# State space branch: the order in program text of a group's norm (third) and the turning of the next group's features (turn)

## The chip, the cores and the metric

The kernel runs on one core of a Trainium2 chip. The metric is the device time of one execution in microseconds (us). An execution is the whole program: two transformer-like layers of a first block and one layer of a second block on 512 tokens of width 1024, in float32.

## The reference, cut to what matters

The change lies in the state space branch of the second block. For 8 groups of 4 heads (head width 64, state width 128, chunks of 128 tokens) the branch computes a decayed, causal sum forwards and backwards, adds a skip term, multiplies by a gate and takes a root-mean-square norm over the 256 features of each group.

```python
def ssd_branch(z, xbc, dt_raw, conv_w, conv_b, dt_bias, a_log, d_skip, norm_g):
    xbc = jax.nn.silu(depthwise_conv_centred(xbc, conv_w, conv_b)).astype(f32)
    xs = xbc[..., :D_INNER].reshape(b, l, SSD_HEADS, SSD_HEAD_DIM)
    Bm = ...; Cm = ...
    y_fwd = ssd_chunked(xs, dt[:, :, 0], A[0], Bm, Cm)
    y_bwd = fl(ssd_chunked(fl(xs), fl(dt[:, :, 1]), A[1], fl(Bm), fl(Cm)))
    y = y_fwd + y_bwd + d_skip.astype(f32)[:, None] * xs
    y = y.reshape(b, l, D_INNER) * jax.nn.silu(z.astype(f32))
    yg = y.reshape(b, l, SSD_GROUPS, D_INNER // SSD_GROUPS)
    yg = yg * lax.rsqrt(jnp.mean(yg * yg, axis=-1, keepdims=True) + EPS)
    y = yg.reshape(b, l, D_INNER) * norm_g.astype(f32)
```

Its result is multiplied by `w_ssd_branch`. Every large product is made of three matmuls on numbers that are split into a rounded high part and a low part.

## The kernel before, in words

All of the work of a stage is written in one text, and a scheduler places every instruction on its engine. It walks a timeline of its own; among instructions that are ready, what stands earlier in the text goes first. So the order of two calls in the text is a preference, and the order on the engines is fixed once the program is built. Each engine then works through its own list strictly in that order, and waits where an operand or a buffer is not there yet.

The branch is written as a class `Group` with five steps, for group g = 0 to 7:

- `feats` (L1267): projections of the group's features from XTh and XTl (matmuls L457 to L459 into a psm bank), and a convolution of each of the four results. The convolution is one ScalarE pass (L1253), four VectorE passes (L1257) and a Silu (L1259).
- `turn` (L1290): for each of four chunks, three TensorE transposes (L1302 twice, L1303) into one pss bank, and two ScalarE copies (L1304 for s.x, L1305 for s.Bt).
- `first` (L1336): four products B times C into the bank s.cb (L1343), then the states. A step of a state is a VectorE product (L1310), a matmul into a pss bank (L1312) and a decayed sum on VectorE (four of L1319, or one copy L1315). `decays` fetches a table of decays by a DMA that GpSimd issues (L1327, into ab), adds and masks it on VectorE (L1329, L1330), takes exponentials on ScalarE (L1332) and multiplies by s.cb (L1333).
- `gate`, `second` (L1358): for each chunk c, matmuls L1368, L1370 and L1381, the sums on VectorE (L1371 to L1382), the product with the gate (L1383), and its squares' sum on ScalarE (L1384). L1384 also overwrites the last use of the chunk's ab buffer, so the next group's DMA into that buffer follows it.
- `third` (L1386): the mean (L510, VectorE), the power -1/2 (L506, GpSimd), four products (L1392), eight transposes (L1394) into two pss banks pts, and the split of both banks (L468 on ScalarE, L469 on VectorE).

There are three psm banks and five pss banks, and a pss bank is given to the next taker when its last reader is done. The branch's output product (L625 adds it to ACC, or L623 copies it) is written behind `feats` of every second group as `ssd_out`, and for the last pair as `ssd_out_group(6)` and `(7)`. Weights come by DMA from SyncE, and are split by L165 (ScalarE) and L167 (VectorE). When `turn` and `third` are called is set by the loop at L1415 to L1429.

Of the kernel before, what the change touches and what calls it, by code (L numbers as in the profile page):

```python
# [246 lines left out]
def body(ctx, tc, I, out, dbg=None, stop=None):  # L247
# [349 lines left out]
    def tok2(w, src, evac, n_k=8):  # L597

        for t in range(NT):
            ps = PM()  # L600
            tk = slice(t * P, (t + 1) * P)
            for k in range(n_k):
                xh, xl = src(k)
                mm3(ps, (xh[:, tk], xl[:, tk]), w[k], k == 0, k == n_k - 1)
            evac(t, ps)
# [15 lines left out]
    def add_to(dst, ps, first):  # L621
        if first:
            nc.scalar.activation(out=dst, in_=ps, func=AF.Copy)  # L623
        else:
            nc.vector.tensor_tensor(out=dst, in0=ps, in1=dst, op=ALU.add)  # L625
# [334 lines left out]
    for j in range(4):  # L960
        heads = []
        for hh in range(2):
            hd = 2 * j + hh
            Z = wk.get("Z", 1024, 4)
            G = wk.get("G", 512, 4)
# [432 lines left out]
    def ssd_out(i):  # L1398
        for u in range(2):
            tok2(WT.get(f"so{i}{u}"), uk, lambda t, ps: add_to(acc[:, t, u * 512:(u + 1) * 512], ps, i == 0), n_k=4)  # L1400

    def ssd_out_group(g):
        for u in range(2):
            w = WT.get(f"so3{g}{u}")
            for t in range(NT):
                ps = PM()
                tk = slice(t * P, (t + 1) * P)
                for k in range(2):
                    uh, ul = uk((2 * g + k) % 4)
                    mm3(ps, (uh[:, tk], ul[:, tk]), w[k], k == 0, k == 1)  # L1410
                add_to(acc[:, t, u * 512:(u + 1) * 512], ps, False)

    G = [Group(g) for g in range(8)]
# [3 lines left out]
    for g in range(8):  # L1417
        G[g].first()
        G[g].gate()
        G[g].second()  # L1420
        if g < 7:
            G[g + 1].feats()
        else:
            ssd_out_group(6)
        if g in (2, 4, 6):
            ssd_out(g // 2 - 1)
        if g < 7:
            G[g + 1].turn()
        G[g].third()  # L1429
    ssd_out_group(7)  # L1430
    for t in range(NT):
        nc.gpsimd.dma_start(h[:, t], hD[t * P:(t + 1) * P, :])
# [238 lines left out]
def kernel_body(tc, I, out, dbg=None, stop=None):  # L1671
    with ExitStack() as ctx:
        body(ctx, tc, I, out, dbg, stop)
# [25 lines left out]
```

## Time and profile before

| what | value |
|---|---|
| time, median of 3 runs | 2582.27 us (2581.29 to 2585.32) |
| the profiled execution's own time | 2581.83 us |
| its span | 2580.1 us |
| TensorE busy, mean granted clock | 2504.9 us (97%), 0.989 |
| VectorE busy | 1714.5 us (66%) |
| ScalarE busy | 1220.2 us (47%) |
| state space branch, from the first table of decays to group 7's norm | about 1357 to 1793 us |
| idle TensorE in 1357 to 1793 us, by the list of waits | 22.5 us |

The span is what the trace covers; the execution's own time is 1.7 us more. Busy is the time in which an engine works on an instruction. A busy TensorE isn't one at full speed: the clock that was granted is listed for each stretch, and 0.50 means 1.2 GHz in place of 2.4 GHz. The matmuls are pipelined, so the distance of two starts tells what one costs.

### The profile page before, as it was taken

What the parts mean: (1) busy time and instruction counts of PE and PEld (TensorE: products, weight loads), DVE (VectorE), ACT (ScalarE), POOL (GpSimd) and SP (SyncE); (2) the same over time, 40 slices, a digit from 0 to 9 for tenths busy, and PEclk for the clock granted to TensorE, in tenths of its full rate; (3) what the DMA queues carried; (4) which work ended last, traced back from release to release, by engine and by line L of the source; (5) the groups of instructions that cost most, each with busy time, mean ns of one, the idle gap of its engine ahead of it and who ended that gap; (6) DMA issues with size and microseconds to landing.
All of it is one profiled execution on the core that took longest, in us unless ns stands there. A gap on an engine that the chain in (4) does not pass through costs nothing. (4 is left out here: it accounts for less than half of the span.)

```text
span 2580.1 us, 33650 instructions
## 1 busy us (share of the span) xinstructions
PE 2504.9 (97%) x12848; PEld 2088.2 (81%) x12848; DVE 1714.5 (66%) x3048; ACT 1220.2 (47%) x2181; POOL 183.5 (7%) x199
## 2 busy tenths in 40 slices
PE   8999999999999989999999999998999999999998
PEld 7888888778888768877888788787887789878877
DVE  5566567775566657577477788887555466487674
ACT  6333345443476554444356554563455436444342
POOL 1100220000201030000121100010000000100000
PEclk9999999999999989999999999998999999999999
DMA  5521235333232133453334333352221233243441
GB/s 175 162 66 61 87 115 169 125 108 129 82 96 89 63 97 113 140 179 98 102 109 125 106 104 109 104 148 77 73 67 40 84 113 123 82 147 104 141 139 58
DMA packets 202001, 278.11 MB, mean 108 GB/s; under 512 B 10800, under 2 KB 127776, under 8 KB 201840
## 3 DMA queue, kind: packets, MB, share of 16 engines
q1 hardware_dynamic: 190352, 236.29, 29.4%
q0 software_dynamic: 10192, 34.96, 5.0%
q10 hardware_dynamic: 1296, 4.72, 0.5%
q8 instruction: 101, 1.65, 0.3%
q14 instruction: 60, 0.49, 0.1%
HBM read 271.56 MB, written 9.61 MB: 109 GB/s over the span
## 5 line engine op out<-in xcount | busy, mean ns | idle before, releaser
L458 PE MATMUL psm<-XTl,hl 128*128 128x512 f32 (+1 forms) x1400 | 537.3, 384 | 7.8 <-DVE XTl L466 7.8
L457 PE MATMUL psm<-XTh,hl 128*128 128x512 f32 (+1 forms) x1400 | 534.5, 382 | 5.9 <-ACT XTh L465 5.1
L459 PE MATMUL psm<-XTh,hl 128*128 128x512 f32 (+1 forms) x1400 | 533.3, 382 | 0.0
L165 ACT ACTIVATE hl<-raw 128x1024 fp32r<-128x1024 f32 x303 | 319.3, 1056 | 313.9 <-PE psm L459 132.6
L167 DVE TENSOR_TENSOR hl<-raw,hl 128x1024 fp32r<-128x1024 f32 x287 | 352.7, 1233 | 149.0 <-ACT hl L165 147.9
L458 PEld LDWEIGHTS psm<-XTl,hl 128*128 128x128 f32 x1400 | 266.3, 190 | 56.9 <-DVE XTl L466 8.6
L457 PEld LDWEIGHTS psm<-XTh,hl 128*128 128x128 f32 x1400 | 265.9, 190 | 55.7 <-ACT XTh L465 6.1
L459 PEld LDWEIGHTS psm<-XTh,hl 128*128 128x128 f32 x1400 | 266.3, 190 | 48.5
L457 PE MATMUL psm<-hl,XTh 128*128 128x512 f32 (+1 forms) x640 | 231.1, 362 | 4.4 <-ACT XTh L465 3.3
L458 PE MATMUL psm<-hl,XTh 128*128 128x512 f32 (+1 forms) x640 | 229.9, 359 | 0.1
L459 PE MATMUL psm<-hl,XTl 128*128 128x512 f32 (+1 forms) x640 | 229.1, 358 | 0.0
L457 PE MATMUL psm<-hl,UAh 128*128 128x512 f32 x368 | 148.6, 405 | 4.9 <-DVE ACC L625 1.5
L458 PE MATMUL psm<-hl,UAh 128*128 128x512 f32 x368 | 144.9, 395 | 0.0
L459 PE MATMUL psm<-hl,UAl 128*128 128x512 f32 x368 | 143.7, 396 | 0.0
L457 PEld LDWEIGHTS psm<-hl,XTh 128*128 128x128 f32 x640 | 122.3, 191 | 21.8 <-ACT XTh L465 3.7
L458 PEld LDWEIGHTS psm<-hl,XTh 128*128 128x128 f32 x640 | 122.2, 191 | 16.6 <-issue 0.5
L459 PEld LDWEIGHTS psm<-hl,XTl 128*128 128x128 f32 x640 | 122.3, 191 | 15.9 <-issue 0.5
L671 ACT ACTIVATE WK<-psm 128x512 f32<-128x512 f32 x66 | 39.5, 598 | 160.8 <-PE psm L459 160.8
L457 PE MATMUL psm<-hl,UBh 128*128 128x512 f32 (+1 forms) x240 | 93.5, 391 | 1.1 <-ACT UBh L468 0.8
L459 PE MATMUL psm<-hl,UBl 128*128 128x512 f32 (+1 forms) x248 | 94.3, 388 | 0.0
L1257 DVE SCALAR_TENSOR_TENSOR WS<-psm,CW,WS 128x511 f32<-128x511 f32 (+1 forms) x120 | 87.5, 740 | 8.7 <-ACT WS L1253 8.4
L458 PE MATMUL psm<-hl,UBh 128*128 128x512 f32 (+1 forms) x240 | 92.2, 386 | 0.0
(481 smaller groups left out, 4839.2 us busy)
## 6 DMA issues: line engine op xcount, KB each, us to landing
raw<-in_mlp_w_down_dram SPq DMA_DIRECT2D x76, 512.0 KB, 3.3
raw<-in_mlp_w_up_dram SPq DMA_DIRECT2D x64, 512.0 KB, 3.9
raw<-in_w_in_dram SPq DMA_DIRECT2D x60, 512.0 KB, 3.7
raw<-in_w_down_dram SPq DMA_DIRECT2D x38, 512.0 KB, 3.9
WS<-aD POOLq DMA_DIRECT2D x32, 512.0 KB, 5.9
raw<-in_w_up_dram SPq DMA_DIRECT2D x32, 512.0 KB, 3.7
raw<-in_w_in_dram SPq DMA_DIRECT2D x33, 256.0 KB, 3.2
raw<-in_a_w_in_dram SPq DMA_DIRECT2D x16, 512.0 KB, 4.9
```

The lines of the kernel that those rows point to most:

```text
L165: s.nc.scalar.activation(out=h, in_=r, func=AF.Copy)
L167: eng.tensor_tensor(out=l, in0=r, in1=h.bitcast(F32), op=ALU.subtract)
L457: nc.tensor.matmul(ps, a[0], b[0], start=first, stop=False, skip_group_check=partial)
L458: nc.tensor.matmul(ps, a[0], b[1], start=False, stop=False, skip_group_check=partial)
L459: nc.tensor.matmul(ps, a[1], b[0], start=False, stop=last, skip_group_check=partial)
L671: nc.scalar.activation(out=rl, in_=ps, func=AF.Relu)
L1257: nc.vector.scalar_tensor_tensor(out=dst[:, o0:o1], in0=ps[:, o0 + d:o1 + d], scalar=cw(j), in1=dst[:, o0:o1], op0=ALU.mult, op1=ALU.add)
```

## The change

The two calls change places in the text of the loop: `third` of group g stands before `turn` of group g + 1.

```diff
         if g in (2, 4, 6):
             ssd_out(g // 2 - 1)
+        G[g].third()
         if g < 7:
             G[g + 1].turn()
-        G[g].third()
     ssd_out_group(7)
```

No instruction is added or taken away by the text, but the scheduler lays the branch out anew from group 0's `second` on, on TensorE, VectorE and ScalarE. The lists of GpSimd and SyncE keep their order. ScalarE's list holds 56 loads of function tables before the change and 46 after it.

The first place is VectorE between group 0's last products and its mean. L1382 and L1383 are the last two steps for a chunk (the rows here are those of chunk 3), L1329 and L1330 belong to the decays of group 1, L1257 to its convolutions, L510 is the mean. Before:

```order
L1329 TENSOR_TENSOR WS<-WS 128x512
L1330 COPY_PREDICATED WS<-masks,WS 128x512
L1310 TENSOR_TENSOR WS<-WS 128x256
L1382 TENSOR_TENSOR WS<-pss,WS 128x256
L1383 TENSOR_TENSOR h<-WS,h 128x256
L1329 TENSOR_TENSOR WS<-WS 128x512
L167 TENSOR_TENSOR hl<-raw,hl 128x1024
L1330 COPY_PREDICATED WS<-masks,WS 128x512
L1257 SCALAR_TENSOR_TENSOR WS<-psm,CW,WS 128x510
L1310 TENSOR_TENSOR WS<-WS 128x256
L1329 TENSOR_TENSOR WS<-WS 128x512
L510 TENSOR_SCALAR ss<-ss 128x4
```

and after the change:

```order
L1329 TENSOR_TENSOR WS<-WS 128x512
L1330 COPY_PREDICATED WS<-masks,WS 128x512
L167 TENSOR_TENSOR hl<-raw,hl 128x1024
L1329 TENSOR_TENSOR WS<-WS 128x512
L1382 TENSOR_TENSOR WS<-pss,WS 128x256
L1330 COPY_PREDICATED WS<-masks,WS 128x512
L1383 TENSOR_TENSOR h<-WS,h 128x256
L1329 TENSOR_TENSOR WS<-WS 128x512
L167 TENSOR_TENSOR hl<-raw,hl 128x1024
L1330 COPY_PREDICATED WS<-masks,WS 128x512
L510 TENSOR_SCALAR ss<-ss 128x4
L1392 TENSOR_SCALAR h<-h,rr 128x256 x4
```

L1382 of chunk 3 stood ahead of group 1's second L1329, and now stands behind it. L1383 moved behind the second L1330. The two L1310, which need the turned features, are gone from between.

The second place is TensorE at the hand-over from group 1 to group 2. Before:

```order
L457 MATMUL psm<-XTh,hl 128x512
L1394 MATMUL pss<-ident,h 128x128 x8
L1343 MATMUL pss<-WS 128x128 x4
L1312 MATMUL pss<-WS 128x256 x2
L458 MATMUL psm<-XTl,hl 128x512
L459 MATMUL psm<-XTh,hl 128x512
```

and after the change (the eight L1394 and three chunks of turn stand 21 matmuls ahead of the piece):

```order
L458 MATMUL psm<-XTl,hl 128x512
L459 MATMUL psm<-XTh,hl 128x512
L1302 MATMUL pss<-ident,WS 128x128 x2
L1303 MATMUL pss<-ident,WS 128x128
L1343 MATMUL pss<-WS 128x128 x4
L1312 MATMUL pss<-WS 128x256 x3
L457 MATMUL psm<-XTh,hl 128x512
L458 MATMUL psm<-XTl,hl 128x512
```

Group 2's features had been turned 47 matmuls ahead of the norm's transposes. Now the last chunk of turn (L1302, L1303) stands directly before L1343 and three of L1312.

The third place is VectorE at the same hand-over: L1310 gives L1312 its operand, L469 is the split of group 1's norm, L1346 reads a product of L1343. Before, ahead of group 1's mean:

```order
L1310 TENSOR_TENSOR WS<-WS 128x256
L1382 TENSOR_TENSOR WS<-pss,WS 128x256
L1383 TENSOR_TENSOR h<-WS,h 128x256
L1329 TENSOR_TENSOR WS<-WS 128x512
L1310 TENSOR_TENSOR WS<-WS 128x256
L1330 COPY_PREDICATED WS<-masks,WS 128x512
L167 TENSOR_TENSOR hl<-raw,hl 128x1024
L1329 TENSOR_TENSOR WS<-WS 128x512
L510 TENSOR_SCALAR ss<-ss 128x4
```

and after the change, behind group 1's L1392:

```order
L469 SCALAR_TENSOR_TENSOR UAl<-pss,COL,UAh 128x512 x2
L1310 TENSOR_TENSOR WS<-WS 128x256
L1257 SCALAR_TENSOR_TENSOR WS<-psm,CW,WS 128x510
L1346 ISA WS,cbd<-pss,ident 128x128
L1346 ISA cbd 128x1
L1257 SCALAR_TENSOR_TENSOR WS<-psm,CW,WS 128x510
L1257 SCALAR_TENSOR_TENSOR WS<-psm,CW,WS 128x511
L1346 ISA WS,cbd<-pss,ident 128x128
L1346 ISA cbd 128x1
L1257 SCALAR_TENSOR_TENSOR WS<-psm,CW,WS 128x510
L1310 TENSOR_TENSOR WS<-WS 128x256
```

The first two L1310 of group 2 stood ahead of L510. They now stand behind L469, with four L1257 of group 3's convolutions and two L1346 between them; the third L1310 comes four L1257 and one L1346 later.

At the end of the branch the output product's matmuls are spread differently. Between the first L1394 of group 6 and the first L1370 of group 7, TensorE's list holds 132 matmuls of L457 to L459 before the change, and 48 after it.

## Rows read from the trace of the kernel before

**Rows 1.** The page, part 1: busy us (share) and instructions of each engine.
```profile
PE 2504.9 (97%) x12848; PEld 2088.2 (81%) x12848; DVE 1714.5 (66%) x3048; ACT 1220.2 (47%) x2181; POOL 183.5 (7%) x199
```

**Rows 2.** Timeline of TensorE: start, us, engine, line, operation, tiles, count, idle before and releaser.
```profile
1375.23 0.39 PE L457 MATMUL psm<-XTh,hl 128*128 128x512 f32 x1
...
1377.95 0.39 PE L457 MATMUL psm<-XTh,hl 128*128 128x512 f32 x1
...
1407.24 1.00 PE L1381 MATMUL pss<-WS 128*128 128x64 f32 x8
...
1425.25 0.66 PE L1394 MATMUL pss<-ident,h 128*128 128x128 f32 x2 [4.51 <-DVE h L1392]
...
1484.59 0.75 PE L1312 MATMUL pss<-WS 128*128 128x256 f32 x2 [2.87 <-DVE WS L1310]
...
1499.45 0.70 PE L1370 MATMUL pss<-WS 128*128 128x256 f32 x2 [1.22 <-DVE WS L1319]
...
1737.20 1.02 PE L1394 MATMUL pss<-ident,h 128*128 128x128 f32 x4 [0.25 <-DVE h L1392]
...
1790.67 1.73 PE L1394 MATMUL pss<-ident,h 128*128 128x128 f32 x7 [3.35 <-DVE h L1392]
```

**Rows 3.** Windows: length, busy us by engine (PE, PEld, DVE, ACT, POOL), PEclk, DMA share, GB/s.
```profile
1420.00:1425.00 5.00, 0.75 (x4) 0.28 (x2) 5.00 (x10) 2.32 (x8) 1.05 (x1) 0.86 0.85 211
1425.00:1430.00 5.00, 4.75 (x19) 4.31 (x20) 5.00 (x13) 1.30 (x4) 0.00 (x0) 0.50 0.34 101
1430.00:1435.00 5.00, 5.00 (x23) 4.18 (x22) 4.32 (x11) 4.52 (x6) 0.00 (x0) 0.96 0.00 0
1485.00:1490.00 5.00, 5.00 (x17) 4.00 (x16) 4.93 (x14) 4.48 (x5) 0.00 (x0) 0.66 0.00 0
```

**Rows 4.** Windows, the hand-overs from group 3 to 4 and from group 4 to 5.
```profile
1568.00:1617.00 49.00, 48.06 (x245) 40.70 (x245) 38.48 (x92) 27.17 (x53) 4.61 (x5) 1.00 0.42 117
1617.00:1675.00 58.00, 55.96 (x270) 46.01 (x269) 50.42 (x107) 32.17 (x59) 4.79 (x5) 1.00 0.37 103
```

**Rows 5.** Timeline of VectorE, group 0's end and group 7's last product.
```profile
1414.59 0.41 DVE L1382 TENSOR_TENSOR WS<-pss,WS 128x256 f32<-128x256 f32 x1
...
1415.04 0.43 DVE L1383 TENSOR_TENSOR h<-WS,h 128x256 f32<-128x256 f32 x1
...
1417.01 0.69 DVE L1329 TENSOR_TENSOR WS<-WS 128x512 f32<-128x512 f32 x1 [1.55 <-DMA WS<-aD]
...
1420.98 0.16 DVE L510 TENSOR_SCALAR ss<-ss 128x4 f32<-128x4 f32 x1
...
1422.37 1.22 DVE L167 TENSOR_TENSOR hl<-raw,hl 128x1024 fp32r<-128x1024 f32 x1
...
1423.50 0.72 DVE L1330 COPY_PREDICATED WS<-masks,WS 128x512 f32<-128x512 uint8 x1
...
1424.77 1.13 DVE L1392 TENSOR_SCALAR h<-h,rr 128x256 f32<-128x256 f32 x4
...
1787.81 0.42 DVE L1383 TENSOR_TENSOR h<-WS,h 128x256 f32<-128x256 f32 x1
```

**Rows 6.** Timeline of ScalarE, the squares of group 0's chunk 3.
```profile
1417.62 0.41 ACT L1384 ACTIVATE WS<-h 128x256 f32<-128x256 f32 x1
```

**Rows 7.** Timeline of GpSimd, the power for group 0.
```profile
1421.23 1.05 POOL L506 TENSOR_TENSOR rr<-ss,mhalf 128x4 f32<-128x4 f32 x1 [1.93 <-DVE ss L510]
```

**Rows 8.** Line L1327, from issue to landing of its DMAs.
```profile
DMA to landing us min/median/max: 5.3/5.9/8.7
```

**Rows 9.** Groups of VectorE, 1357 to 1793 us: count, busy us, mean ns, idle before.
```profile
L1257 DVE SCALAR_TENSOR_TENSOR WS<-psm,CW,WS 128x511 f32<-128x511 f32 (+1 forms) x112 | 81.7, 740 | 0.9 <-ACT WS L1253 0.6
L167 DVE TENSOR_TENSOR hl<-raw,hl 128x1024 fp32r<-128x1024 f32 x58 | 70.5, 1217 | 19.9 <-ACT hl L165 19.8
L1319 DVE SCALAR_TENSOR_TENSOR WS<-WS,pss 128x64 f32<-128x64 f32 x128 | 27.1, 272 | 0.0
```

**Rows 10.** Groups of ScalarE, the same stretch, one load of a function table.
```profile
L1332 ACT ACT_TABLE_LOAD x18 | 23.1, 1283 | 3.5 <-DMA WS<-aD 3.2
```

## Prediction

> **What bounds the kernel now.** I read the page first: TensorE is busy for 2504.9 of 2580.1 us [rows 1], so only its idle time and its slow stretches can be won. The windows by hand-over and the list of TensorE's waits in the branch, 1357 to 1793 us, came next, and then TensorE's timeline, for each place where it sat idle [rows 2]. The 3.35 us before the last norm lie behind group 7, whose text doesn't change. The reader is to see that the loss sits where one group hands over to the next, and that VectorE is named as the releaser. Group 0's norm is waited for 4.51 us, the states of group 2 for 2.87 and 1.22 us [rows 2]. The window of the hand-over from group 3 to 4 lacks 0.94 us, that from 4 to 5 lacks 2.04 us [rows 4]. After the 4.51 us the clock reads 0.50 for 5 us, and part of the windows beside them: 0.86 is 1.4 us, 0.96 is 0.4 us at the lower level, 1.2 GHz. Of these 6.8 us some 5.2 had work in them, which cost 2.6 us; the 3.4 us of low clock in 1485 to 1490 (0.66) cost 1.7 us [rows 3]. All that could be won in front of group 7 is some 16 us.
>
> **The unit prices.** Twelve matmuls start between 1375.23 and 1377.95 [rows 2]: 0.227 us each. On VectorE consecutive starts are closer than the durations: L167 lasts 1.22 and the next starts after 1.13 us [rows 5]. I take 0.08 us off each: L1257 0.66, L167 1.13, L1319 0.19 [rows 9], a 512-wide row 0.61 (L1329), L1330 0.64, a 256-wide one 0.33 (L1382), four L1392 1.05 [rows 5].
>
> **The change part by part.** It adds and removes no work of TensorE, VectorE, GpSimd or SyncE. What moves is order, so each hand-over has to be laid out again.
>
> *Group 0's norm.* All rows up to chunk 2 stay. The second L1329 starts at 1417.01, held for 1.55 us by its DMA [rows 5]; that DMA starts when L1384 of chunk 1 is done, which stays, and landings take 5.3 to 8.7 us [rows 8]. L1382 of chunk 3 started at 1414.59, L1383 at 1415.04 [rows 5]. Now both stand behind this L1329: L1382 at 1417.6, L1330 at 1417.9, L1383 at 1418.6, some 3.5 us later than before. Two ScalarE steps follow (four L1332 that need this L1330, then L1384, which started at 1417.62 before [rows 6]): the sum is there at 1420.4. VectorE has L1329, L167 and L1330 ahead of L510: 1418.9 + 0.61 + 1.13 + 0.64 = 1421.3. The power takes 0.25 + 1.05 us (1420.98 to 1422.28 before [rows 5, 7]): L1392 at 1422.7, and L1394 0.48 us behind it, as before [rows 2, 5], at 1423.2. The saving is that four L1257 and two L1310, 3.3 us, no longer stand between; the loss is the wait for the DMA. TensorE gets there after L1381 of chunk 2 at 1407.24 [rows 2], 19 matmuls, the last L1381 and 26 matmuls: 1407.24 + 1.0 + 4.3 + 1.0 + 5.9 = 1419.4. It waits 3.8 us in place of 4.5, and the clock falls as it did. Gain 0.7 us.
>
> The Trainium skill (DMA: Bandwidth & Descriptors, "Anatomy of one DMA — SWDGE (gpsimd) path") puts such a DMA at about 2.0 us plus its bytes at 436 GB/s, by estimate 3.2 us for 512 KB. By it the L1329 wouldn't hold L1382, and this wait would shrink by up to 2.7 us more. The landings above are longer, so I don't count that.
>
> *Group 1's second pair of L1312.* From group 0's L1392 to the fourth L1310 VectorE has 13 L1257, 4 L1310, 4 L1333, 2 L469, L1329, L1330, L167, 4 L1346 (taken as 256-wide) and the four L1392: 8.6 + 1.3 + 2.4 + 1.3 + 0.6 + 0.6 + 1.1 + 1.3 + 1.1 = 18.3 us. TensorE has 24 transposes and L1343, at 1/8 us each as the 8 of L1381 in 1.00 us [rows 2], 24 matmuls, two L1312 (0.5), 21 matmuls, and 2.6 us for the clock, begun 0.5 us late: 0.5 + 3.0 + 5.4 + 0.5 + 4.8 + 2.6 = 16.8. A new wait of 1.5 us.
>
> *Group 1 to 2.* The norm is early: 57 matmuls stand between the last L1381 and L1394, against 47. But the norm's two banks and three chunks of turn fill the five pss banks, so the fourth chunk takes a bank that L469 frees, and L1343 follows it. Three L1312 stand directly behind. The first L1346 can't start before L1343, and to the second L1310 there are 2 L1346, 4 L1257 less the one ahead, and L1310: 0.3 + 2 x 0.66 + 0.3 + 0.66 + 0.33 = 2.9 us, while TensorE has 0.6 us of L1343 left. Wait 2.3 us. To the third L1310 it is 4 L1257, L1346 and L1310, 3.3 us, less two L1312 (0.5): 2.7 us more. Of this I have no row; the bounds are nothing, where VectorE's convolutions are done before L1343, and the longest wait of such a kind, 4.51 us [rows 2], for each of the two. I take 5.0, near the 2.87 us row twice, with the clock cost of that row, 1.7. That is 6.7 us, against 2.87 + 1.22 + 1.7 = 5.8 before: a loss of 0.9 us.
>
> *Groups 2 to 5.* L1394 stands 42, 51, 50 and 48 matmuls behind the last L1381 (9.5 to 11.6 us). Laid out as for group 0, with the same L1329 in the way, L1392 is ready 2 to 3 us earlier than that. Between L1343 and the first L1312 there are 24 matmuls, 5.4 us, over the 2.9 us just found. So I put these waits at nothing; the cover that hides the new chain (L1394, L468, L469, L1302, L1304, L1310) is 21 to 25 matmuls ahead of L1302 and these 24, and if it is gone each costs up to 4.5 us. The 0.94 and 2.04 us [rows 4] go: gain 3.0 us.
>
> *Group 6 to the end.* Here the cover is used up. Behind the first L1394 of group 6, at 1737.20 with 0.25 us of idle [rows 2], TensorE had 132 output matmuls left, now 48. So it gets there 84 x 0.227 = 19.1 us later, less 0.9 us of turn that isn't yet done: 1736.95 + 18.2 = 1755.1. From there the end hangs on VectorE: 17 rows of 512 (10.4), L1330 0.6, 4 L167 (4.5), 30 rows of 256 (9.9), 16 L1319 (3.1), 4 L1346 (1.2), small ones 0.2, four L1392 1.1: 31.0 us to the last L1383. TensorE's own work there is some 19 us. Add 2.4 us in which L1329 waits for the DMA that follows L1384 of chunk 3, and 2.9 us from the last L1383 to L1394, 1787.81 to 1790.67 [rows 5, 2]: 36.3 us, 1791.4. Before it was 1790.67 [rows 2]. A loss of 0.7 us. Its lower bound is without the DMA's wait, 2.4 less; its upper one has ScalarE and TensorE steps in between that VectorE must wait for, up to 8 us more.
>
> *ScalarE's table loads.* Ten fewer, at 1.28 us [rows 10]: 12.8 us of an engine that isn't the bound. I count nothing. The Trainium skill (ScalarE: Activation LUTs, "What ACT_TABLE_LOAD costs") says 2.66 us for a switch with its drain, by estimate 26.6 us; the trace shows the load alone, and by both the sum stays.
>
> *Sum.* -0.7 + 1.5 + 0.9 - 3.0 + 0.7 = -0.6 us, from 2581.83 us of the profiled execution (span 2580.1 and 1.7 around it): 2581.2. The median is 0.4 us above that execution, so I put the time at 2581.6.
>
> **The rivals.** *The hand-overs come clean.* If VectorE's convolutions of group 3 are done before L1343, the 6.7 us of group 1 to 2 and the 1.5 us fall away: 2581.6 - 8.2 = 2573.4. For it: L1392 has lost 3.3 us of other work ahead of it, and ScalarE 12.8 us. Against it: the order puts those L1257 behind the L1346 that has to wait.
>
> *The end without cover.* Slower: behind group 6 the whole chain from norm to norm lies bare, since 48 matmuls are 10.9 us for 36 us of chain. Every stop counts in full: the DMA at 8.7 in place of 5.9 us [rows 8] (2.8); L1304 stands on ScalarE behind the exponentials of chunk 3, which wait for the same DMA (by estimate 3 us more); and the clock falls under the last products (by estimate 2 us, near the 1.7 and 2.6 found above). It decides from 41 us of chain on: 2581.6 + 8 = 2589.6. For it: TensorE already waits 3.35 us for the last norm [rows 2]. Against it: VectorE's list is short there, and I have counted the first DMA's wait.
>
> *The change does little.* The hand-overs swap their waits one for one; that is the forecast's neighbourhood, not a case of its own. That the order isn't changed at all is out, as the three pieces show.
>
> **How the numbers follow.** Chances: forecast 0.48, clean hand-overs 0.25, bare end or a hand-over of groups 2 to 5 that loses its cover 0.27. A measurement of this kernel can tell 0.2%, 5.2 us. The forecast's own range, 2577 to 2586, lies within that. The range of 8 in 10 goes from 2573 (clean) to 2590 (bare end). Faster takes the clean case and a little of the rest, 0.25; same 0.48; slower 0.27.
>
> **What would show it.** Right: an idle of some 4 us before group 0's L1394 with L1382 of chunk 3 behind an L1329 that waits for its DMA; an idle before the L1312 of group 2; none before L1394 in groups 2 to 5; some 15 us of idle TensorE between L1394 of group 6 and of group 7. Wrong: no idle there, L1394 of group 0 before 1421, or new waits for L469 or L1304 in the middle groups.

## The result, and the profile after

The changed kernel takes 2610.97 us (median of 4 runs, 2603.67 to 2611.21) against 2581.78 us of the kernel before on the same chip: a ratio of 1.0105, 95% interval 1.0087 to 1.0122. It is 29 us slower. The forecast was 2581.6 us, its range 2573 to 2590 us, so the time lies outside. The profiled execution took 2611.21 us, span 2609.4 us.

The page of the changed kernel, part 1, the row that answers to [rows 1]:

```profile
PE 2514.3 (96%) x12848; PEld 2093.5 (80%) x12848; DVE 1718.3 (66%) x3048; ACT 1207.5 (46%) x2171; POOL 185.0 (7%) x199
```

The work is the same. The DMAs of L1327 take about as long to land, 5.5/6.0/8.7 us against 5.3/5.9/8.7 [rows 8]. ScalarE has less to do: 14 table loads of 1.28 us at L1332 in place of 18 [rows 10]. The time is lost on TensorE inside the branch. Windows of TensorE from one group's first L1394 to the next group's, the kernel before, then the changed one (length, busy us, matmuls, granted clock, DMA share, GB/s):

```profile
1357.00:1425.25 68.25, 61.36 (x310) 0.99 0.49 132
1425.25:1473.46 48.21, 48.21 (x232) 0.95 0.28 72
1473.46:1528.89 55.43, 51.33 (x250) 0.97 0.48 136
1528.89:1580.95 52.06, 52.06 (x263) 1.00 0.37 102
1580.95:1630.22 49.27, 46.68 (x234) 1.00 0.43 123
1630.22:1691.49 61.27, 60.88 (x297) 1.00 0.40 108
1691.49:1737.20 45.71, 45.46 (x230) 1.00 0.46 133
1737.20:1790.67 53.47, 45.05 (x209) 0.92 0.30 84
sum 433.67, PE 411.03; mean PE 51.38
```

```profile
1357.00:1425.92 68.92, 61.23 (x306) 0.99 0.47 128
1425.92:1485.19 59.27, 54.42 (x256) 0.95 0.32 87
1485.19:1541.66 56.47, 49.07 (x231) 0.91 0.41 109
1541.66:1601.73 60.07, 60.07 (x297) 1.00 0.32 87
1601.73:1662.92 61.19, 54.29 (x254) 0.94 0.41 122
1662.92:1722.29 59.37, 59.37 (x294) 1.00 0.33 88
1722.29:1782.19 59.90, 55.14 (x259) 0.94 0.44 139
1782.19:1820.68 38.49, 27.62 (x134) 0.83 0.22 62
sum 463.68, PE 421.22; mean PE 52.65
```

The last norm comes 30.0 us later (463.68 less 433.67), which is the whole loss. 19.8 us of it are idle time (42.46 less 22.64), 10.2 us are busy time. Of these about 1 us is work that had slipped past 1357 us (2031 matmuls in these windows against 2025; over the whole execution TensorE is busy for 9.4 us more). The rest is the same work at a lower clock (0.83 to 0.95 in five windows). The second line of each table begins at group 0's norm, the third at group 1's, and so on. In the changed kernel the windows behind the norms of groups 0, 1, 3 and 5 lack 4.85, 7.40, 6.90 and 4.76 us (length less busy time); those behind groups 2 and 4 lack nothing.

TensorE's waits in the branch, the kernel before and the changed one (tile, line, releaser: us, times, longest):

```profile
PE pss L1394 <- DVE h L1392: 8.1, 3, 4.5
PE pss L1312 <- DVE WS L1310: 3.8, 2, 2.9
...
PE psm L457 <- DVE WS L1257: 2.3, 2, 1.5
```

```profile
PE pss L1394 <- DVE h L1392: 8.4, 3, 4.4
PE psm L457 <- DVE WS L1257: 7.9, 5, 2.5
PE pss L1302 <- DVE UAl L469: 6.9, 3, 3.0
PE pss L1312 <- DVE WS L1310: 6.9, 6, 3.4
PE pss L1302 <- ACT WS L1305: 3.3, 1, 3.3
```

The waits for the norm (L1394) didn't change. New are those of the turning (L1302) for the split (L469) and for its own copies (L1305). Longer are those that come later: of the states (L1312), and of matmuls whose bank a late convolution (L1257) holds. That these too follow from the late turning is argued from the order of the lists, and not shown wait by wait.

The hand-over from group 1 to 2 in the changed kernel, on GpSimd, ScalarE, VectorE and TensorE (start, us, what, idle before and releaser):

```profile
1482.68 0.88 POOL L1327 DMA_DIRECT2D WS<-aD  x1 [9.46 <-ACT WS L1384]
```

```profile
1481.90 0.40 ACT L1384 ACTIVATE WS<-h 128x256 f32<-128x256 f32 x1
...
1490.89 1.28 ACT L1332 ACTIVATE WS<-WS 128x128 f32<-128x128 f32 x4 [6.38 <-DVE WS L1330]
...
1493.02 1.24 ACT L468 ACTIVATE UAh<-pss,COL 128x512 fp32r<-128x512 f32 x2
1494.16 0.37 ACT L1304 ACTIVATE WS<-pss 128x256 f32<-128x256 f32 x1
```

```profile
1484.69 1.14 DVE L1392 TENSOR_SCALAR h<-h,rr 128x256 f32<-128x256 f32 x4 [1.15 <-POOL rr L506]
1489.37 0.69 DVE L1329 TENSOR_TENSOR WS<-WS 128x512 f32<-128x512 f32 x1 [3.54 <-DMA WS<-aD]
...
1494.29 1.41 DVE L469 SCALAR_TENSOR_TENSOR UAl<-pss,COL,UAh 128x512 fp32r<-128x512 f32 x2
```

```profile
1485.19 1.13 PE L1394 MATMUL pss<-ident,h 128*128 128x128 f32 x8 [0.66 <-DVE h L1392]
...
1495.09 0.44 PE L1302 MATMUL pss<-ident,WS 128*128 128x128 f32 x2 [2.98 <-DVE UAl L469]
...
1499.91 2.04 PE L1312 MATMUL pss<-WS 128*128 128x256 f32 x4 [3.37 <-DVE WS L1310]
```

Read it as one chain. The squares L1384 of chunk 3 end at 1482.3 and let the last table of decays be fetched (1482.68). VectorE's list has L1329 of that table next, and stands until 1489.37. ScalarE's list has the exponentials (L1332) of that table ahead of the split, and stands for 6.38 us, though the transposes that the split reads were done at 1486.3. Only then come the split (L468, L469) and, behind it on ScalarE, the copies of the turning (L1304). TensorE has the transposes of norm and turning, 1.9 us, and 21 matmuls, 5.0 us, and then the fourth chunk of the turning wants a sixth pss bank: it stands until L469 gives one back.

The hand-over from group 3 to 4 has the same stop on TensorE, but another one on ScalarE ahead of it:

```profile
1611.21 0.44 PE L1302 MATMUL pss<-ident,WS 128*128 128x128 f32 x2 [2.69 <-DVE UAl L469]
```

```profile
1606.14 1.06 ACT L165 ACTIVATE hl<-raw 128x1024 fp32r<-128x1024 f32 x1 [3.47 <-DMA raw<-in_w_ssd_branch_dram]
...
1609.70 1.24 ACT L468 ACTIVATE UAh<-pss,COL 128x512 fp32r<-128x512 f32 x2
```

The norm's transposes are done at 1602.8 here. ScalarE stands at the split of weights (L165) until their DMA has landed, then loads a function table (1607.22, 1.28 us), takes the exponentials (1608.52), and only then comes to L468. From group 5 to 6 it is the same: L165 waits 1.93 us for weights, and L1302 waits 1.27 us for L469. Behind groups 2 and 4, L1302 waits for nothing.

### The profile page after: what moved, and what is told of

It is laid out like the page before. It is cut to its first block, busy times and chain, and to the rows that moved or that the text cites. A ratio compares the mean times of both kernels' runs of the same rounds, so it can differ in the third digit from the quotient of the medians.

```text
span 2609.4 us, 33635 instructions
## 1 busy us (share of the span) xinstructions
PE 2514.3 (96%) x12848; PEld 2093.5 (80%) x12848; DVE 1718.3 (66%) x3048; ACT 1207.5 (46%) x2171; POOL 185.0 (7%) x199
## 5 line engine op out<-in xcount | busy, mean ns | idle before, releaser
L457 PE MATMUL psm<-XTh,hl 128*128 128x512 f32 (+1 forms) x1400 | 535.3, 383 | 8.7 <-ACT XTh L465 5.1
L459 PE MATMUL psm<-XTh,hl 128*128 128x512 f32 (+1 forms) x1400 | 531.9, 381 | 0.0
L165 ACT ACTIVATE hl<-raw 128x1024 fp32r<-128x1024 f32 x303 | 319.5, 1057 | 307.1 <-PE psm L459 138.0
L457 PEld LDWEIGHTS psm<-XTh,hl 128*128 128x128 f32 x1400 | 265.8, 190 | 59.1 <-ACT XTh L465 6.1
L459 PEld LDWEIGHTS psm<-XTh,hl 128*128 128x128 f32 x1400 | 266.1, 190 | 48.7
L457 PE MATMUL psm<-hl,XTh 128*128 128x512 f32 (+1 forms) x640 | 230.7, 361 | 7.1 <-ACT XTh L465 3.5
L459 PE MATMUL psm<-hl,XTl 128*128 128x512 f32 (+1 forms) x640 | 229.0, 358 | 0.0
L457 PE MATMUL psm<-hl,UAh 128*128 128x512 f32 x368 | 150.8, 411 | 5.8 <-DVE ACC L625 2.6
L459 PE MATMUL psm<-hl,UAl 128*128 128x512 f32 x368 | 145.9, 402 | 0.0
L457 PEld LDWEIGHTS psm<-hl,XTh 128*128 128x128 f32 x640 | 121.9, 191 | 25.0 <-ACT XTh L465 3.9
L459 PEld LDWEIGHTS psm<-hl,XTl 128*128 128x128 f32 x640 | 122.0, 191 | 16.1 <-issue 0.5
L457 PE MATMUL psm<-hl,UBh 128*128 128x512 f32 (+1 forms) x240 | 94.3, 394 | 1.1 <-ACT UBh L468 0.8
L459 PE MATMUL psm<-hl,UBl 128*128 128x512 f32 (+1 forms) x248 | 94.3, 388 | 0.0
L1257 DVE SCALAR_TENSOR_TENSOR WS<-psm,CW,WS 128x510 f32<-128x510 f32 (+1 forms) x120 | 86.6, 743 | 8.8 <-ACT WS L1253 8.5
```

The lines of the kernel that those rows point to most:

```text
L165: s.nc.scalar.activation(out=h, in_=r, func=AF.Copy)
L457: nc.tensor.matmul(ps, a[0], b[0], start=first, stop=False, skip_group_check=partial)
L459: nc.tensor.matmul(ps, a[1], b[0], start=False, stop=last, skip_group_check=partial)
L1257: nc.vector.scalar_tensor_tensor(out=dst[:, o0:o1], in0=ps[:, o0 + d:o1 + d], scalar=cw(j), in1=dst[:, o0:o1], op0=ALU.mult, op1=ALU.add)
```

## The experiments

Three explanations were on record. *Late split* (theory 1 in the texts below; with the banks alone, the bank theory): the split, and what stands behind it, is late because it stands behind the decays of chunk 3 in the lists of VectorE and ScalarE; TensorE feels it through the banks. *Late decays* (rival 2): the transfers themselves hold VectorE. *The turning behind the norm* (rival 3): TensorE misses the turning as work to do while the norm is made. The numbers in brackets are the 95% interval of the ratio to the kernel before. An edit makes the scheduler lay out the rest of the branch anew, with one exception below.

**One order fixed on VectorE: the split ahead of chunk 3's decays.**

```diff
-            nc.vector.tensor_tensor(out=T, in0=T, in1=vw(dlt[:, c, hs:hs + 4], 0, [[1, 4], [0, P]]), op=ALU.add)
+            with tc.issue_after(G[g - 1].last.ins) if g > 0 and c == 3 else ExitStack():
+                nc.vector.tensor_tensor(out=T, in0=T, in1=vw(dlt[:, c, hs:hs + 4], 0, [[1, 4], [0, P]]), op=ALU.add)
```

`last` is the second L469 of a group; the lines that keep it are left out here.

> The changed kernel, with one order fixed: VectorE issues the add L1329 of chunk 3's decays only after the two subtractions of the group's split (L469). Theory 1 (late split): in the changed kernel the split stands behind the decays of chunk 3, whose transfer L1327 starts only after the squares L1384 of chunk 3, so TensorE's fourth turning (L1302) waits 2.7 to 3.0 us for L469 and the first matmul of the states (L1312) 3.4 us after it. It expects the waits of L1302 on L469 to fall from 6.9 us to under 2 and the time from 2611 to between 2585 and 2597. Rival 2 (late decays): the transfers themselves are late and hold VectorE, whatever stands behind them; then the decays now come later still and the time stays at 2605 to 2615. Rival 3 (the turning itself comes too late behind the norm): 2605 to 2611, with the wait moved from L469 to L1392 or L1310.

2595.76 us [1.0037 to 1.0070]: 15.2 of the 28.5 us back that the change costs (2610.97 less 2582.5, the kernel before in these runs). Its hand-over from group 1 to 2, VectorE and TensorE (L1330, L1393, L1395 are the lines L1329, L1392, L1394 of the other kernels):

```profile
1482.75 1.40 DVE L469 SCALAR_TENSOR_TENSOR UAl<-pss,COL,UAh 128x512 fp32r<-128x512 f32 x2
1484.07 0.68 DVE L1330 TENSOR_TENSOR WS<-WS 128x512 f32<-128x512 f32 x1
```

```profile
1479.41 1.13 PE L1395 MATMUL pss<-ident,h 128*128 128x128 f32 x8 [0.38 <-DVE h L1393]
...
1486.17 0.38 PE L1302 MATMUL pss<-ident,WS 128*128 128x128 f32 x2
```

L469 starts 3.3 us behind the first of the transposes instead of 9.1, and no L1302 in the branch waits for it. The late split is part of the cause; the rest, 13 us, isn't explained by it.

**The norm's banks taken from the other pool.** `pts = [PM(), PM()]` in place of `[PS(), PS()]`.

> The changed kernel, with the two banks of the norm's transposes (L1390) taken from the pool of three large-product banks (PM) instead of the pool of five (PS), so that the four turnings never wait for a bank that the norm holds. Theory 1 (late split, felt through the banks): no wait of L1302 on L469; 2585 to 2597 us, unless feats or the products wait for the PM banks instead (L457 or L1257 up by over 5 us). Rival 2 (late decays): the turning comes early, but L1375 and L1343 still wait for the decays, and the time stays above 2603. Rival 3 (the turning behind the norm): L1302 still starts only after L1394, waits of L1312 on L1310 as long as now (6.9 us in six), above 2603.

2633.09 us [1.0183 to 1.0213]. No waits for L469, but two of 9.25 and 9.64 us at L1343 for the Silu L1259, and 14.6 us at L457: the whole schedule came out otherwise, with norms 47 and 83 us apart in turn. It doesn't tell the theories apart.

**Five buffers for the decays.** `wk.get("ab", 1024, 5)` in place of 4.

> The changed kernel with five buffers instead of four for the decays (L1326), so that the transfer of chunk 3 needn't wait for the squares of the same chunk. Rival 2 (late decays): VectorE's waits of L1329 for the transfer fall from 47 us by half and the time goes to 2582 to 2592. Theory 1 (late split): the split is no longer late where the transfer has landed; L1302 waits under 2 us for L469 in all; 2585 to 2597. Rival 3 (the turning behind the norm): 2603 to 2611.

2603.14 us [1.0066 to 1.0096]: 7.8 us back. VectorE still waits 51.9 us for the tables (47.3 in the changed kernel) and L1302 still 6.6 us for L469. So neither theory's reason for a gain holds, and where the 7.8 us come from stays open.

**The squares L1384 in a buffer of their own.** `out=wk.get("sq", 256, 2)` in place of `out=t2`.

> The changed kernel, with the squares L1384 written to a small buffer of their own instead of into the decays' buffer, so that the transfer into that buffer is released by VectorE's add L1382 and not by ScalarE's squares, which came 4.5 us after L1383 between groups 1 and 2. Theory 1 and rival 2: the transfer of chunk 3 starts some 3 to 5 us earlier, the split follows it, L1302 waits under 3 us for L469 in all; 2588 to 2600. Rival 3: 2605 to 2611.

2611.93 us [1.0100 to 1.0130]: nothing back. The table at group 1's end is fetched at 1475.60 instead of 1482.68, as meant. But in the new layout its L1329 stands ahead of the norm's L1392, and the wait has only changed its place. TensorE's first row of waits:

```profile
PE pss L1394 <- DVE h L1392: 15.0, 5, 5.9
```

It was 8.4 us. L1302 waits for L469 once, 3.7 us, in place of 6.9 in three. A miss for both theories as they stood: an earlier transfer, with the layout that came with it, is worth nothing.

**Only the norm ahead, transposes and split behind the turning.**

```diff
             ssd_out(g // 2 - 1)
+        G[g].norm()
         if g < 7:
             G[g + 1].turn()
```

This edit is against the kernel before: `norm` has the mean, the power and the four L1392, and `third`, still behind `turn`, keeps the transposes and the split.

> One part of the change alone: the mean, the power and the four scalings (L1392) of the norm stand ahead of the turning, but the transposes (L1394) and the split (L468, L469) stay behind it as in the kernel before. Theory 1 (late split, felt through the banks): what costs the time is that the transposes take two of the five banks ahead of the turning and that the turning's last chunk waits for the split; with the turning first again, no L1302 waits for L469 and the time is 2576 to 2590. Rival 3 (the turning comes too late because it stands behind the norm, on VectorE and ScalarE as well): the norm is still in front on VectorE, and part of the loss stays: 2592 to 2605.

2581.07 us [0.9985 to 1.0004]. In the trace TensorE, VectorE, ScalarE and GpSimd work through the same instructions in the same order as in the kernel before. So this run is that kernel again: `norm` uses VectorE and GpSimd, `turn` TensorE and ScalarE, and their order in the text decides nothing. What an earlier norm on VectorE would cost isn't tested by it. It does say that the new layout, and with it the loss, comes only with the new place of the transposes and the split.

**The turning in three banks.** x of two chunks in one bank, all Bt in another.

> The changed kernel, with the turning's results packed in three banks instead of four (the x of two chunks in one bank, the Bt of all four in another). Two banks of the norm and three of the turning fill the pool of five, so L1302 needn't wait for L469; the next to ask for a bank is the product of the keys (L1343), which takes the one that the split frees. Bank theory with the wait only moved: L1343 waits 2 to 3 us for L469 in the place of L1302, the turning's copies run beside it, 2600 to 2611. Bank theory in full (the count of banks is the loss, and one bank less cures it): 2585 to 2597. Rival 3 (the turning behind the norm): 2605 to 2611.

2619.16 us [1.0126 to 1.0156], 8 us slower than the change itself. Chunks that share a bank wait for one another's copies (L1302 and L1303 for L1304 and L1305: 7.0 us in five). No transpose of the turning and no L1343 waits for L469 any more, and the loss is still there. That speaks against the bank theory in full, but not cleanly, as the waits for the shared banks are new. A miss.

**Split first and five buffers together.**

> Two earlier edits of the changed kernel together: the split ordered ahead of the decays of chunk 3 (alone 2595.8 us) and five buffers for the decays (alone 2603.1 us). If the two losses are apart (a late split, and late transfers that hold VectorE), their gains of 15.2 and 7.8 us add up to 2588 or less. If five buffers helped only by bringing the split earlier, nothing is left for them to gain here, and the time is 2593 to 2597.

2607.04 us [1.0080 to 1.0110]: the two gains don't add up, 11 us of the first are lost. Between groups 0 and 1 the add for chunk 2's table, which the edit doesn't order, now stands ahead of the split and waits 2.92 us for its transfer.

**Odd and even groups apart.** `third` ahead of `turn` only where g is odd, or only where it is even.

> The kernel before, with the norm ahead of the turning only for odd groups (1, 3, 5; group 7 has no turning). The waits of L1302 for L469 in the changed kernel stand at the hand-overs behind groups 1, 3 and 5 (2.98, 2.69 and 1.27 us). If the loss is one of single hand-overs, by these waits and what follows them, the odd swaps carry most of the 29 us: 2600 to 2607. If every swapped hand-over costs alike (rival 3: the turning behind the norm, 29 us over seven hand-overs), three of seven make 2592 to 2597. If the loss comes only where all are swapped (each turning late makes the next norm late), under 2590.

> The kernel before, with the norm ahead of the turning for even groups only (0, 2, 4, 6). The odd groups alone cost 11.2 us. If the hand-overs add up to the 29 us of the whole change: 2598 to 2602. If every swapped hand-over costs alike (3.7 us each by the odd ones): 2596 to 2599. If the hand-overs without a product stage beside them (behind groups 0 and 6 above all) carry it: over 2602; if the losses come of swaps that follow each other: under 2594.

Odd: 2593.68 us [1.0026 to 1.0056], 11.2 us for three hand-overs. Even: 2596.29 us [1.0039 to 1.0069], 13.9 us for four. Together 25.1 of the 28.5 us, on average 3.7 and 3.5 us each. That each single hand-over costs alike isn't shown. In the kernel with the odd ones swapped, the windows behind groups 1, 3 and 5 have 9.2 us of idle time, against 6.9 before; the branch has 30.2 us, against 22.6. Most of what was added, 5.3 of 7.6 us, stands in other windows, behind group 0 (2.7 us) and group 6 (2.0 us) above all. So the place where TensorE stands still isn't the only place that caused it.

**Six and two banks instead of five and three**, in the changed order and in the old one.

> The changed kernel with the eight PSUM banks divided 6 and 2 (small results and large products) instead of 5 and 3, so that two banks of the norm and four of the turning are there together. To be read against the kernel before with the same division. Bank theory (the turning's fourth chunk waits for the bank that the late split frees): no wait of L1302 on L469, and the changed order is at most 15 us slower than the old one at this division (29 at 5 and 3). Theory of the chain (turning, copies, L1310 and the first states now come one after the other behind the norm's transposes, whatever banks there are): L1302 no longer waits for L469, but the loss against the old order stays at 20 to 30 us. Two banks for the products alone may cost both kernels some time.

> The kernel before with the PSUM banks divided 6 and 2; the ground for the changed kernel at this division. All theories: 2580 to 2620, by what the third bank of the large products is worth; no wait of L1302 on L469.

2637.13 us against 2630.78 us: the changed order loses 6.3 us here, not 28.5. TensorE waits for L469 at no L1302. That speaks for the banks, but weakly: the third bank of the products is worth 48 us, and on that ground other waits hide some. The chain still shows, as waits of the states (L1312 for L1310): 14.7 us in the changed order and 3.5 in the old one.

**The split ahead of chunk 2's decays too.** `c >= 2` in place of `c == 3`.

> The changed kernel with the split (L469) ordered ahead of the decays of chunk 2 as well as of chunk 3 (chunk 3 alone: 2595.8 us). If what is left of the loss (13 us) is VectorE's waits for the decays' transfers ahead of the split, it falls to 2584 to 2592. If it is the chain of turning, copies and first states behind the norm, the time stays at 2593 to 2600.

2603.60 us [1.0070 to 1.0100], slower than with chunk 3 alone. VectorE's waits for the tables fall to 33.6 us, below the 35.2 us of the kernel before, and the time is 21 us above it. So the sum of these waits doesn't set the time, which speaks against the late decays. It is also above what either theory expected. Among TensorE's waits one of 7.5 us at L1312 is new.

**The norm between the halves of the turning.**

```diff
+        if g < 7:
+            G[g + 1].turn(0, 2)
         G[g].third()
         if g < 7:
-            G[g + 1].turn()
+            G[g + 1].turn(2, 4)
```

> The norm with its transposes and its split between the second and the third chunk of the turning. Two banks of the norm and the third chunk's fill the pool of five, and the fourth chunk takes the bank of the first, which two copies free: the transposes and the split still stand ahead of half the turning, but no bank that the split frees is waited for. Bank theory: 2578 to 2588, no wait of L1302 on L469. Theory of the chain (the turning has to come early, while TensorE waits for the norm on VectorE, ScalarE and GpSimd, and the copies, L1310 and the first states follow it): about half of the loss stays, 2590 to 2600.

2578.59 us [0.9975 to 0.9994]: the whole loss is gone, and 3.7 us more. Transposes and split still stand ahead of half the turning; by the count of banks the fourth chunk can take the one that the first chunk's copies freed long before. No L1302 (here L1303) waits for L469. The states still wait for their operand (L1313 for L1311, 7.3 us in three), so the chain isn't gone; the idle time of the branch, 21.8 us, is that of the kernel before (22.6).

**The norm behind the next group's first stage.** `G[g - 1].third()` behind `G[g].first()`.

> The change carried on in the other direction: the kernel before with the norm, its transposes and its split not only behind the next group's turning but behind its whole first stage (states and decays). If the loss comes from what stands behind the norm's transposes and split, nothing waits behind them any more, and the time is 2570 to 2582. If the place behind the turning is late enough already, 2580 to 2584; if the products of the group (L457 on UAh) then wait for the split, over 2590.

2583.94 us [0.9994 to 1.0013]: still later brings nothing.

**The two helpful edits on the old order**, five buffers and the split first.

> The kernel before with five buffers for the decays, the edit that took 7.8 us off the changed kernel. If VectorE's waits for the decays' transfers (35 us in the kernel before) cost time by themselves: 2572 to 2580. If they cost only where the split stands behind them and TensorE behind the split: 2580 to 2585.

> The kernel before with the split ordered ahead of the decays of chunk 3, the edit that took 15.2 us off the changed kernel. Late split felt through the banks: in the old order nothing asks for the norm's banks so soon, so 2579 to 2586. If a late split costs in itself (the products of L457 wait for it): 2570 to 2578.

2586.27 us [1.0007 to 1.0026] and 2579.97 us [0.9981 to 1.0000]. What gave 7.8 and 15.2 us back in the changed order costs 4.0 and gives 2.3 here: most of what they gave came of what the change had made.

**ScalarE's order set by hand.** The turning's copies of chunks 0 and 1 ahead of L468 and of chunk 3's exponentials.

```diff
+                if s.g > 0 and c == 1:
+                    for i in G[s.g - 1].his:
+                        tc.add_manual_dep(i, bt.ins.name, mybir.DependencyInfo(mybir.DependencyClass.NoSync, mybir.DependencyReason.DATA), reason="copies first")
...
-            for q in range(4):
-                nc.scalar.activation(out=T[:, q], in_=T[:, q], func=AF.Exp, bias=nb[:, c, hs + q:hs + q + 1])
+            with tc.issue_after(s.c1) if c == 3 else ExitStack():
+                for q in range(4):
+                    nc.scalar.activation(out=T[:, q], in_=T[:, q], func=AF.Exp, bias=nb[:, c, hs + q:hs + q + 1])
```

`bt` is the copy L1305, `s.c1` that of the second chunk, and `his` holds the two L468 of a group; the lines that keep them are left out here.

> The changed kernel with ScalarE's order alone set by hand: behind groups 0 to 6 the turning's copies of the first two chunks (L1304, L1305) come ahead of the split's L468 and of the exponentials of chunk 3's decays. On TensorE the norm's transposes still stand ahead of the whole turning. The two copies free two banks and give VectorE the features of chunks 0 and 1 early. If the loss is the place of the split and of the decays in front of the turning's copies (the bank that the fourth chunk waits for is one effect of it): no long wait of L1302 on L469, 2580 to 2592. If the transposes' own place on TensorE costs (the turning late behind the norm): 2598 to 2611.

2589.85 us [1.0021 to 1.0046]: 21.1 of 28.5 us back. Group 1 to 2, on ScalarE, VectorE and TensorE (L1338 is L1332, L1334 is L1329, L1400 is L1394):

```profile
1484.82 0.38 ACT L1304 ACTIVATE WS<-pss 128x256 f32<-128x256 f32 x1 [1.23 <-PE pss L1303]
...
1485.68 1.29 ACT L468 ACTIVATE UAh<-pss,COL 128x512 fp32r<-128x512 f32 x2
1488.87 0.70 ACT L1338 ACTIVATE WS<-WS 128x128 f32<-128x128 f32 x2 [1.90 <-DVE WS L1335]
```

```profile
1487.35 0.69 DVE L1334 TENSOR_TENSOR WS<-WS 128x512 f32<-128x512 f32 x1 [3.39 <-DMA WS<-aD]
...
1491.31 1.42 DVE L469 SCALAR_TENSOR_TENSOR UAl<-pss,COL,UAh 128x512 fp32r<-128x512 f32 x2
```

```profile
1483.32 1.14 PE L1400 MATMUL pss<-ident,h 128*128 128x128 f32 x8 [0.70 <-DVE h L1398]
...
1489.63 0.38 PE L1302 MATMUL pss<-ident,WS 128*128 128x128 f32 x2
```

VectorE waits for the table as before, 3.39 us, and its L469 is late. TensorE has the same order at this hand-over, the norm's transposes ahead of the whole turning, but for 19 matmuls instead of 21 ahead of the fourth chunk; elsewhere its list came out otherwise, and VectorE's too. The copies start 1.5 us behind the first of the transposes instead of 9.0, and L468 too is past before the exponentials. So a bank is free, and the fourth turning doesn't wait. What is left of waits is the states' (3.9 us at this hand-over).

**Both edits that beat the kernel before.** Halves, and the split ahead of chunk 3's decays.

> The norm between the two halves of the turning (alone 2578.6 us, 3.7 less than before) together with the split ordered ahead of the decays of chunk 3 (2.3 less than before when done to the old order). If the split still stands behind a late transfer in the halved turning and holds the first states (L1311 to L1313, 7.3 us of waits), 2573 to 2577. If it isn't waited for any more: 2577 to 2581.

2578.22 us [0.9970 to 0.9989], 4.5 us faster than the kernel before. That it beats the halves alone (2578.59) can't be told.

## Why the prediction was wrong

*The step that failed* is "Groups 2 to 5 ... I put these waits at nothing", a gain of 3.0 us. The idle time of the four windows that begin at their norms grew from 3.2 to 11.7 us (6.90 and 4.76 in two of them), and two of them ran at 0.94, by estimate up to 7 us more (0.06 of 61.19 and of 59.90 us). The idle time is 8.4 of the 19.8 us of new idle time; 4.9 stand behind group 0, 3.3 behind group 1, 2.5 behind group 6 and 0.8 ahead of group 0's norm. The prediction had the chain (L1394, L468, L469, L1302, L1304, L1310) by name, and its cover of 21 to 25 matmuls. It then held against the cover VectorE's rows from L1343 to L1310 alone, 2.9 us.

ScalarE's list wasn't walked. There the split stood behind exponentials whose table is fetched only when L1384 is done (group 1 to 2), or behind an L165 that waits for weights and a table load (groups 3 to 4 and 5 to 6). From the first L1394 (1601.73) to the fourth turning (1611.21) it is 9.5 us from group 3 to 4, and 9.9 us from group 1 to 2 (1485.19 to 1495.09), of which the transposes cover 1.8 and 1.9 and the 21 matmuls 4.8 and 5.0.

Of the 11.7 us, 2.69 and 1.27 are L1302's waits for L469; the others are at L1312 (2.5 us), L457 for L1257 (2.9) and L457 for a sum of the output product, L625 (2.3). The sign that the prediction had set for being wrong, "new waits for L469 or L1304 in the middle groups", came. The prediction had just this stop for group 6 ("L1304 stands on ScalarE behind the exponentials"), as a rival's extra.

*Group 0's norm* was right in its mechanism: L1382 of chunk 3 stands behind an L1329 that waits for its DMA. VectorE there (answers to [rows 5]):

```profile
1419.04 0.69 DVE L1329 TENSOR_TENSOR WS<-WS 128x512 f32<-128x512 f32 x1 [1.31 <-DMA WS<-aD]
1419.65 0.42 DVE L1382 TENSOR_TENSOR WS<-pss,WS 128x256 f32<-128x256 f32 x1
...
1421.74 0.69 DVE L1329 TENSOR_TENSOR WS<-WS 128x512 f32<-128x512 f32 x1 [0.72 <-DMA WS<-aD]
...
1425.42 1.14 DVE L1392 TENSOR_SCALAR h<-h,rr 128x256 f32<-128x256 f32 x4 [1.17 <-POOL rr L506]
```

L1392 came at 1425.42 instead of 1422.7: the L1329 that "stays" at 1417.01 came 2.0 us later, and the next one waited 0.72 us for a DMA of its own; TensorE's wait is 4.4 us, as before [rows 2], and the gain of 0.7 us nothing.

*Group 1's second pair of L1312* (1.5 us) was mis-placed: no such wait, but 4.85 us of idle in that window, 1.71 and 2.48 of it at matmuls that a late convolution holds. *Group 1 to 2* was forecast at 5.0 us of waits and 1.7 us for the clock. The waits are 2.98 and 3.37, and 1.04 at the next L1312, 7.4 us; the L1302 had no price. The clock's part was too small:

```profile
1495.00:1500.00 5.00, 1.53 (x12) 0.66 0.37 106
1500.00:1505.00 5.00, 3.96 (x9) 0.50 0.00 0
1505.00:1510.00 5.00, 5.00 (x20) 0.81 0.00 0
```

Behind these stops the level 1.2 GHz lasts for some 10 us, against 3.4 us in the kernel before [rows 3].

*Group 6 to the end* was nearly right in itself: 38.5 us from the first L1394 to group 7's, forecast 36.3. But it began at 1782.19 instead of 1755.1. *The table loads*: ten fewer gave nothing that can be seen, as the prediction had it. But a load isn't free where it stands in the chain, as the one at 1607.22, 1.28 us, stands ahead of the split.

*The rivals.* The bare end was on the slower side, and its condition named "a hand-over of groups 2 to 5 that loses its cover", but its price, 8 us, was that of the end alone. Four lost covers at the 4.5 us that the prediction itself gives them would have been 18 us. The range ended at 2590.

*What is shown and what isn't.* That the loss comes with the new place of transposes and split is shown, since without it the lists stay as they were. What the place of the norm's own work costs isn't tested. That half the turning ahead of the transposes cures the loss is shown (2578.59). That ScalarE's order carries most is shown by one kernel (21.1 of 28.5 us), with a reserve: the scheduler lays out the rest anew, and edits that differ little moved the time by 8 us (split first for chunk 3, or for 2 and 3) and 11 us (with a fifth buffer). What the last 7 us of that kernel are, and what five buffers gained, stays open.

The table of chunk 3 was issued at 1482.68, and the L1329 that reads it started at 1489.37, 6.7 us later, with nothing else ahead of it. The Trainium skill (DMA: Bandwidth & Descriptors, "Anatomy of one DMA — SWDGE (gpsimd) path") gives by estimate 3.2 us for such a DMA, and by that VectorE's 3.54 us at L1329 would have been nearly nothing; the trace disagrees, here as in [rows 8].

## What to carry to other kernels

When a program is laid out anew, walk every in-order list between a result and its reader, not only the engine named as releaser: what stands ahead of the split on ScalarE, and what that waits for, made most of the loss here. Count a pool's banks over the moved pair: two and four out of five mean that the last taker can depend on the slowest reader of the first. Price a lost cover at every repetition (28.5 us over seven hand-overs here), not once. And before an experiment is read, compare the engines' lists: an edit of the text can leave them as they were.

## What the runs showed of the hardware

The lower clock adds to a wait: 19.8 us more idle time came with some 9 us more busy time for the same matmuls, so a wait priced by its idle time alone leaves out about a third of the loss in this branch. And a bank moved from the products to the small results costs the old order 48 us (2630.78 against 2582.41), more than the whole change.
